# Two feed-forwards whose later blocks multiply with normed activations instead of norming the products

## The chip, the cores and the metric

The kernel runs on one core of a Trainium2 chip. The metric is the time of one execution in microseconds, the median of three runs. The kernel is one program for five engines, named as in the profile: PE (matrix products, with PEld for loading weights), DVE (vector work), ACT (activation functions and copies), POOL (GpSimd) and SP (which issues the weight transfers). Each engine works through its own list in order and waits on semaphores for what others make.

## The reference, cut to what matters

256 tokens of width 1024 go through a first block (feed-forward, attention mixers, feed-forward, a gate) and then through a second block of two layers. Each layer of the second block ends as follows, and the change lies in the gate and up products here:

```python
def swiglu_ffn(x, w_gate, w_up, w_down):
    return (jax.nn.silu(x @ w_gate) * (x @ w_up)) @ w_down

y = memory_cross_attention(x, mem_n, xa_wq[l], xa_wk[l], xa_wv[l], xa_wo[l])
x = layer_norm(ALPHA * x + y, ln_xa_g[l], ln_xa_b[l])
y = swiglu_ffn(x, ffn_wg[l], ffn_wu[l], ffn_wd[l])
x = layer_norm(ALPHA * x + y, ln_ffn_g[l], ln_ffn_b[l])
```

The hidden width of the feed-forward is 2816. Everything is float32.

## The kernel before, in words

Activations lie transposed: a tile holds 128 channels on the partitions and the 256 tokens along the free axis, so the 1024 channels are 8 tiles. A weight matrix is cut into 128x128 tiles, and an out block j is the sum over 8 weight tiles. The gate and up matrices are interleaved: even j is a gate block, odd j the up block beside it, 44 blocks for a layer. To keep float32 accuracy with fast products each operand is cut into a rounded part `hi` and a rest `lo`, and each weight tile takes three matmuls: weight hi by activation hi, weight hi by activation lo, weight lo by activation hi. The prediction calls these three a triple; a block is 8 triples.

Weights stream in units of 8 tiles. In `get`, called once a unit, ACT rounds the unit four ahead (L309, `hi<-raw`) and DVE makes the rest of the unit three ahead (L333, `lo<-raw,hi`, 128x1024). `get` also runs one step of a background generator, and `tick` runs the next step of every delayed piece of work. The lists of all engines are thus fixed by this one program, unit by unit; nothing is ordered again later.

The norm ahead of the feed-forward is deferred. While the sum z = ALPHA x + y of a channel tile comes out of the attention, `Norm.add` makes `xs`, which is z times the gain, in two parts, plus two further columns with gain and bias: 258 columns. The products of the gate and up blocks start on `xs` at once, before mean and variance are known. With a delay of two units the statistics are gathered, and in the fifth unit of the stage two tiles come ready, `rows`: the reciprocal deviation and minus the scaled mean, spread over the partitions. Blocks 0 to 3 wait in PSUM until then; the matmuls of block 4 come right behind the transposes that make `rows`. From then on each block is finished by `evac`: ACT copies the two further columns (L679), DVE multiplies the product by the one row (L680) and adds the other (L681); for a gate block ACT then takes Silu (L1896), for an up block DVE multiplies it with the gate (L1902), and the result is cut in two by ACT (L436) and DVE (L437).

The residual of the next norm needs the normed x itself. `Norm.values` makes it in the background, one channel tile k in three units: DVE multiplies z by the one row (L693) and adds the other (L694), ACT applies gain and bias (L696).

Line numbers here and in the rows are those of the kernel before; in the changed kernel the same lines stand 5 higher up to `Norm.values` (L680 is L685), 6 higher inside it, and 31 higher in the last of them (L1902 is L1933).

Of the kernel before, what the change touches and what calls it, by code (L numbers as in the profile page):

```python
# [9 lines left out]
F32 = mybir.dt.float32  # L10
F32R = mybir.dt.float32r
U32 = mybir.dt.uint32
AF = mybir.ActivationFunctionType
ALU = mybir.AluOpType
# [3 lines left out]
T = 256  # L18
D = 1024
NB = D // P  # L20
# [162 lines left out]
class Net:  # L183
    def __init__(self, tc=None, aps=None, order=None, dbg=None):
        self.dry = tc is None
        self.order = [] if self.dry else order
        self.packers = {}
        self.pos = 0
        self.prepped = 0
        self.rested = 0  # L190
        self.delayed = []
        self.eager = False
        self.half = {}
        self.loaded = 0
        self.ready = {}
        self.raws = {}
        self.bg = deque()
        self.dbg = dbg
        if self.dry:
            self.nc = self.tc = NULL  # L200
            self.aps = {k: NULL for k in ("xT", "pT", "memT", "vec0", "vec", "const", "bias", "wts", "out")}
            self.pe = self.ve = self.ac = self.po = NULL
        else:
            self.tc, self.nc, self.aps = tc, tc.nc, aps
            self.pe, self.ve, self.ac, self.po = (
                tc.nc.tensor, tc.nc.vector, tc.nc.scalar, tc.nc.gpsimd)
            self.chunks = chunks_of(order)
            self.chunk_of = {}
            for c, (units, _, _) in enumerate(self.chunks):
                for u in units:  # L210
                    self.chunk_of[u] = c
# [139 lines left out]
        for _ in self.gen_B(*a, **k):  # L351
            pass

    def gen_T(self, name, tiles, src, x, evac, w=T, whole=(), xf=None):


        left = {}
        for j, k in tiles:
            left[j] = left.get(j, 0) + 1
        seen = set()  # L360
        self.packers[name] = lambda inp, u: np.concatenate(
            [src(inp, j, k) for j, k in tiles[8 * u:8 * u + 8]], axis=1)
        acc = {}
        for t, (j, k) in enumerate(tiles):
            if t % 8 == 0:
                hi, lo = self.get(name, t // 8, P * min(8, len(tiles) - t), t // 8 in whole)
            if j not in acc:
                acc[j] = self.ps("acc")
            c = 128 * (t % 8)
            o = acc[j][:, :w]  # L370
            first, last = j not in seen, left[j] == 1
            seen.add(j)
            left[j] -= 1
            if t // 8 in whole:
                self.mm(o, hi[:, c:c + P], xf[k], start=first, stop=last)
            else:
                xk = x(k) if callable(x) else x[k]
                self.mm(o, hi[:, c:c + P], xk[:, :w], start=first, stop=False)
                self.mm(o, hi[:, c:c + P], xk[:, w:2 * w], start=False, stop=False)
                self.mm(o, lo[:, c:c + P], xk[:, :w], start=False, stop=last)  # L380
            if last:
                evac(j, o)
                del acc[j]
            if t % 8 == 7 or t + 1 == len(tiles):
                yield
# [251 lines left out]
class Norm:  # L637
# [5 lines left out]
    def __init__(self, net, name, off=0, delay=1, over=1.0):  # L643
        self.delay = delay
        self.net, self.g, self.b, self.off = net, name + "_g_2", name + "_b_2", off
        self.stats = Stats(net, NB, LN_EPS / over ** 2, True, TAIL_N)
        self.pend = None
        self.xs, self.keep = {}, {}

    def add(self, k, z):  # L650
        n, ve, ac, po = self.net, self.net.ve, self.net.ac, self.net.po
# [29 lines left out]
        ve.scalar_tensor_tensor(t, NM, c[:, 0:1], t, ALU.mult, ALU.add)  # L681
        return t, c[:, 1:2]

    def values(self, pace=1):

        n, ve, ac = self.net, self.net.ve, self.net.ac
        for k in range(NB):
            while not self.rows.ready:
                yield
            R, NM = self.rows.rb  # L690
            x = n.St("x")
            z = self.stats.z[k]
            ve.tensor_tensor(x, z, R, ALU.mult)  # L693
            ve.tensor_tensor(x, x, NM, ALU.add)  # L694
            g, b = n.vec(self.g, self.off + k), n.vec(self.b, self.off + k)
            n.later(lambda x=x, g=g, b=b: ac.activation(x, x, AF.Identity, scale=g, bias=b))  # L696
            self.keep[k] = x
            for _ in range(pace):
                yield

# [1156 lines left out]
def second_block(n, H, xs, KT, V, filler, lb):  # L1859
    ac, ve, po, pe = n.ac, n.ve, n.po, n.pe  # L1860

    def residual(X, norm, scale=None):
        def evac(j, o):
            z = n.St("z")
            if scale is None:
                ve.scalar_tensor_tensor(z, X[j], ALPHA, o, ALU.mult, ALU.add)  # L1866
            else:
                ve.scalar_tensor_tensor(z, o, scale[:, j:j + 1], X[j], ALU.mult, ALU.add)
            norm(j, z)
        return evac  # L1870

    X = {k: H[k] for k in range(NB)}
    for l in range(2):

        ln = Norm(n, "ln_mix", l * NB, D_MIX[l], ALPHA if l else 1.0)
        if l == 0:
            yo, late = hybrid(n, X, xs, filler, lb)
            late()
            n.stream_T("abo", row_tiles(NB, NB, A_HEAD), lambda inp, j, k: cut(w2(inp, "ab_w_out_2"), k, j),
                       yo, residual(X, ln.add))  # L1880
        else:
            sc = n.st("psc", 8)
            po.tensor_scalar(sc, n.vec("pool_scale_2", 0, NB), 1.0 / ALPHA, None, ALU.mult)
            pool_mixer(n, X, xs, residual(X, ln.add, sc), filler)
        filler.through(l)
        nx = Norm(n, "ln_xa", l * NB, D_XA)
        cross(n, l, ln, KT[l], V[l], residual(ln.keep, nx.add))
        X = ln.keep
        n.debug("mix%d" % l, [X[k] for k in range(NB)])
        ln = nx  # L1890
        hd, held = {}, {}

        def evac(j, o):
            t, c = ln.apply(o, "s", ac.copy)
            if j % 2 == 0:
                act = once(lambda: ac.activation(t, t, AF.Silu, bias=c))  # L1896
                n.later(act)
                held[j // 2] = t, act
            else:
                s, act = held.pop(j // 2)  # L1900
                act()
                ve.scalar_tensor_tensor(s, t, c, s, ALU.add, ALU.mult)  # L1902
                hd[j // 2] = n.split_later(s, name="hd")

        n.bg.append(ln.values(3))
        n.stream_T("g%d" % l, row_tiles(2 * NF, NB, G_HEAD),
                   lambda inp, j, k, l=l: cut(w2(inp, ("ffn_wg_2", "ffn_wu_2")[j % 2], l), k, j // 2),
                   ln.xs, ln.rows.after(evac), Norm.W)
        n.settle()
        n.flush_bg()  # L1910
        X = ln.keep
        n.debug("xa%d" % l, [X[k] for k in range(NB)])
        st = n.stats(NB, LN_EPS, True, TAIL_D[l])
        n.stream_T("d%d" % l, row_tiles(NB, NF), lambda inp, j, k, l=l: cut(w2(inp, "ffn_wd_2", l), k, j),
                   hd, residual(X, lambda j, z: st.add(z)))
        if l == 0:
            keep = {}
            for k in range(NB):
                keep[k] = n.St("xp", 272)
                po.memset(keep[k][:, 0:16], 0.0)  # L1920
            lz = Lazy(n, st, "ln_ffn_g_2", "ln_ffn_b_2", 0,
                      keep={k: keep[k][:, 16:272] for k in range(NB)})
            lz.start(lambda: filler.fill(F_POOL[0]))
            xs = (lz, keep)
            X = lz.keep
        else:
            rm = st.norm_cols()
            R, M, nm = n.ps("pb"), n.ps("pb"), n.St("nm")
            n.bcast(R[:, :T], rm)
            n.bcast(M[:, :T], rm[:, 2:4])  # L1930
            ac.copy(nm, M[:, :T])
            ts = {}

            def finish(k):
                add = po if k in POOL_ADDS else ve
                add.tensor_tensor(ts[k], ts[k], nm, ALU.add)
                x = n.St("x")
                ac.activation(x, ts[k], AF.Identity, scale=n.vec("ln_ffn_g_2", NB + k),
                              bias=n.vec("ln_ffn_b_2", NB + k))
                n.nc.sync.dma_start(out=n.aps["out"][:, k * T:(k + 1) * T], in_=x)  # L1940

            for k in range(NB):
                ts[k] = n.St("nt")
                ve.tensor_tensor(ts[k], st.z[k], R[:, :T], ALU.mult)
                if k > 1:
                    finish(k - 2)
            finish(NB - 2)
            finish(NB - 1)
# [128 lines left out]
```

## Time and profile before

| what | us |
|---|---|
| median of three runs | 1269.68 (1269.11 to 1271.19) |
| the profiled execution | 1269.32 |
| its span in the trace | 1267.4 |
| PE busy in the span | 1246.4 |
| DVE busy | 954.4 |
| ACT busy | 702.0 |
| POOL busy | 106.2 |

The 1.9 us between the execution's time and its span lie around the first and last instruction. A busy time is the union of an engine's instructions. A PE instruction's record lasts longer than the distance to the next one, since matmuls overlap; the pace is read from the starts. The two gate and up stages run from about 758 to 887 us and from about 1063 to 1191 us of the span.

### The profile page before, as it was taken

The numbers are of one execution on the slowest core, as the hardware profiler recorded it, in microseconds if no ns is written. First come the engines' busy times: TensorE is split into PE (matmuls) and PEld (weight loads), VectorE is DVE, ScalarE is ACT, GpSimd is POOL, SyncE is SP. The second block draws the span as 40 slices with busy tenths as digits, with TensorE's granted clock in tenths as the row PEclk, the third lists the DMA queues.
The fourth block names the chain that finished last, engine by engine and source line by source line (L and its number), as shares of the span: only waits on it lengthen the run. The fifth ranks groups of instructions, "written<-read, shape, count | busy, mean of one in ns | idle before, by whom it ended". The sixth has DMA issues, their size and how long they took to land.

```text
span 1267.4 us, 23973 instructions
## 1 busy us (share of the span) xinstructions
PE 1246.4 (98%) x9748; PEld 1206.7 (95%) x9748; DVE 954.4 (75%) x1749; ACT 702.0 (55%) x1269; POOL 106.2 (8%) x232
## 2 busy tenths in 40 slices
PE   8999999999999999999999999999999999999996
PEld 8999998879999999998889999999999899999996
DVE  6778656875766567679999778998558868998753
ACT  6656546566644454464466675655445676565532
POOL 1001002500000000000012120000003030000000
PEclk9999999999999999999999999999999999999998
DMA  8645555431455545544344334555544425355541
GB/s 295 224 170 205 202 182 194 156 128 67 167 180 187 191 177 198 195 172 150 116 167 167 133 127 146 198 197 191 209 167 162 172 101 200 130 194 179 203 161 34
DMA packets 32589, 215.15 MB, mean 170 GB/s; under 512 B 3872, under 2 KB 5152, under 8 KB 7776
## 3 DMA queue, kind: packets, MB, share of 16 engines
q1 hardware_dynamic: 31680, 211.28, 45.9%
q0 software_dynamic: 800, 2.36, 0.5%
q8 instruction: 76, 1.25, 0.4%
q14 instruction: 33, 0.27, 0.1%
HBM read 212.57 MB, written 1.05 MB: 169 GB/s over the span
## 4 chain that ended last, share of the span: by engine, by line
PE 92%; DVE 4%; ACT 2%; DMA 1%; issue 0%; POOL 0%; SPq 0%; ACTq 0%; DVEq 0%
PE acc L344 75%; PE accB L344 5%; PE vB L344 3%; PE kT L344 3%; PE S L344 1%; DVE lo L333 1%; DMA raw<-wts 1%; PE pv L344 1%; PE oM L344 1%; PE pt L992 1%; PE O L344 0%; ACT E L976 0%; ACT hi L309 0%; DVE sb L969 0%; PE ds L344 0%
## 5 line engine op out<-in xcount | busy, mean ns | idle before, releaser
L344 PE MATMUL acc<-xs,hi 128*128 128x256 f32 (+1 forms) x3392 | 613.3, 283 | 1.5 <-ACT hi L309 0.8
L344 PEld LDWEIGHTS acc<-xs,hi 128*128 128x128 f32 x3392 | 524.3, 189 | 2.6 <-ACT hi L309 1.1
L333 DVE TENSOR_TENSOR lo<-raw,hi 128x1024 fp32r<-128x1024 f32 (+2 forms) x395 | 472.2, 1211 | 10.0 <-ACT hi L309 9.5
L344 PE MATMUL acc<-xs,lo 128*128 128x256 f32 (+1 forms) x1696 | 478.4, 282 | 0.8 <-DVE lo L333 0.8
L309 ACT CAST hi<-raw 128x1024 fp32r<-128x1024 f32 (+2 forms) x395 | 403.2, 1039 | 35.9 <-DMA raw<-wts 14.1
L344 PEld LDWEIGHTS acc<-xs,lo 128*128 128x128 f32 x1696 | 322.6, 190 | 1.2 <-DVE lo L333 1.2
L344 PE MATMUL acc<-hd,hi 128*128 128x256 f32 x1408 | 249.6, 281 | 0.0
L344 PEld LDWEIGHTS acc<-hd,hi 128*128 128x128 f32 x1408 | 215.5, 188 | 0.0
L344 PE MATMUL acc<-hd,lo 128*128 128x256 f32 x704 | 197.2, 280 | 0.0
L344 PEld LDWEIGHTS acc<-hd,lo 128*128 128x128 f32 x704 | 132.6, 188 | 0.0
L344 PE MATMUL acc<-yo,hi 128*128 128x256 f32 x512 | 92.9, 283 | 0.3 <-ACT yo L443 0.2
L436 ACT CAST hd<-s 128x256 fp32r<-128x256 f32 x88 | 35.8, 407 | 103.4 <-DVE s L791 58.0
L344 PEld LDWEIGHTS acc<-yo,hi 128*128 128x128 f32 x512 | 78.9, 188 | 1.0 <-ACT yo L443 0.5
L344 PE MATMUL acc<-yo,lo 128*128 128x256 f32 x256 | 71.9, 281 | 0.0
L344 PE MATMUL accB<-hi,xs 128*128 128x512 f32 (+1 forms) x192 | 59.8, 393 | 0.0
L512 ACT ACTIVATE sq<-z 128x256 f32<-128x256 f32 x48 | 19.6, 407 | 68.7 <-DVE z L1866 68.7
L680 DVE TENSOR_TENSOR s<-acc,rows 128x256 f32<-128x256 f32 x88 | 37.0, 421 | 20.2 <-ACT c L679 20.2
L1866 DVE SCALAR_TENSOR_TENSOR z<-x,acc 128x256 f32<-128x256 f32 x32 | 13.2, 418 | 51.5 <-PE acc L344 51.5
L760 ACT ACTIVATE xs<-h,vt 128x256 fp32r<-128x256 f32 x24 | 12.2, 510 | 69.0 <-DVE h L803 66.9
L1573 DVE SCALAR_TENSOR_TENSOR cv<-up,vt,cv 128x256 f32<-128x256 f32 x120 | 50.0, 479 | 0.0
L344 PEld LDWEIGHTS acc<-yo,lo 128*128 128x128 f32 x256 | 48.2, 188 | 0.0
L589 POOL TENSOR_TENSOR r<-m,mhalf 128x2 f32<-128x2 f32 x8 | 12.0, 1503 | 420.9 <-DVE m L588 420.9
(306 smaller groups left out, 1479.9 us busy)
## 6 DMA issues: line engine op xcount, KB each, us to landing
raw<-wts SPq DMA_DIRECT2D x193, 1024.0 KB, 4.8
raw<-wts SPq DMA_DIRECT2D x6, 512.0 KB, 8.6
raw<-wts SPq DMA_DIRECT2D x2, 832.0 KB, 4.3
x<-xT SPq DMA_DIRECT2D x4, 256.0 KB, 6.5
mem<-memT POOLq DMA_DIRECT2D x8, 128.0 KB, 4.8
bias<-bias POOLq DMA_DIRECT2D x4, 256.0 KB, 3.1
out<-x SPq DMA_DIRECT2D x8, 128.0 KB, 1.9
raw<-wts SPq DMA_DIRECT2D x1, 768.0 KB, 4.1
```

The costliest lines, as they stand in the source:

```text
L309: self.ac.copy(hi[:, c], raw[:, c])
L333: self.ve.tensor_tensor(lo[:, c], raw[:, c], hi[:, c].bitcast(F32), ALU.subtract)
L344: self.pe.matmul(out, a, b, start=start, stop=stop, **k)
L436: self.later(lambda: self.ac.copy(hi, src), lambda: self.ve.tensor_tensor(xs[:, T:], src, hi.bitcast(F32), ALU.subtract))
L512: self.net.ac.activation(sq, z, AF.Square)
L589: net.po.tensor_tensor(r[:, 0:2], m[:, 2:4], net.mhalf[:, :2], ALU.pow)
L680: ve.tensor_tensor(t, o[:, :T], R, ALU.mult)
L760: ac.activation(hi, h, AF.Copy, scale=g)
L992: n.pe.transpose(o[:, kb * T + t * P:kb * T + (t + 1) * P], E[:, t * T + kb * P:t * T + (kb + 1) * P], n.ident)
L1573: ve.scalar_tensor_tensor(a, u[:, k:k + T], w, a, ALU.mult, ALU.add)
L1866: ve.scalar_tensor_tensor(z, X[j], ALPHA, o, ALU.mult, ALU.add)
```

## The change

`Norm.values` now works on POOL in the two feed-forwards (the attention keeps DVE), and one channel tile a unit instead of one in three. Behind it two more steps are queued for each tile: ACT rounds the normed x to `xn` hi (L706), and DVE makes its lo part (L709). Once all eight tiles have passed through the list, `pick` gives the next pair of blocks `xn` instead of `xs`: 256 columns, nothing to norm behind them. ACT then takes Silu straight from PSUM (L1919) and DVE multiplies from PSUM (L1922).

```diff
@@ Norm
-    def values(self, pace=1):
+    def values(self, split=False):
         n, ve, ac = self.net, self.net.ve, self.net.ac
+        add = n.po if split else ve
         for k in range(NB):
             while not self.rows.ready:
                 yield
...
-            ve.tensor_tensor(x, z, R, ALU.mult)
-            ve.tensor_tensor(x, x, NM, ALU.add)
+            add.tensor_tensor(x, z, R, ALU.mult)
+            add.tensor_tensor(x, x, NM, ALU.add)
             g, b = n.vec(self.g, self.off + k), n.vec(self.b, self.off + k)
-            n.later(lambda x=x, g=g, b=b: ac.activation(x, x, AF.Identity, scale=g, bias=b))
+            steps = [lambda x=x, g=g, b=b: ac.activation(x, x, AF.Identity, scale=g, bias=b)]
+            if split:
+                xn = n.Tt("xn", F32R)
+                hi = xn[:, :T]
+                steps.append(lambda x=x, hi=hi: ac.copy(hi, x))
+                def low(x=x, hi=hi, xn=xn, k=k):
+                    ve.tensor_tensor(xn[:, T:], x, hi.bitcast(F32), ALU.subtract)
+                    self.normed[k] = xn
+                steps.append(low)
+            n.later(*steps)
             self.keep[k] = x
-            for _ in range(pace):
-                yield
+            yield
+    def pick(self, j):
+        if j % 2 == 0:
+            self.late = len(self.normed) == NB
+        return (self.normed, T) if self.late else (self.xs, self.W)
@@ second_block
         def evac(j, o):
+            if late[j]:
+                if j % 2 == 0:
+                    s = held[j // 2] = n.St("s")
+                    ac.activation(s, o, AF.Silu)
+                else:
+                    s = held.pop(j // 2)
+                    ve.tensor_tensor(s, s, o, ALU.mult)
+                    hd[j // 2] = n.split_later(s, name="hd")
+                return
             t, c = ln.apply(o, "s", ac.copy)
...
-        n.bg.append(ln.values(3))
+        n.bg.append(ln.values(True))
```

In the list of PE the new operand begins with block 14 in both layers, so that 30 of the 44 blocks are 256 columns wide. The last rows of block 13 and the first of block 14 in the first layer, before:

```order
L344 MATMUL acc_9774<-xs_9193,hi_9614 128x258 x2
L344 MATMUL acc_9774<-xs_9193,lo_9656 128x258
L344 MATMUL acc_9774<-xs_9235,hi_9614 128x258 x2
L344 MATMUL acc_9774<-xs_9235,lo_9656 128x258
L344 MATMUL acc_9817<-xs_9018,hi_9654 128x258 x2
L344 MATMUL acc_9817<-xs_9018,lo_9694 128x258
```

The same six rows now, where `xn_9460` is the normed tile k = 0:

```order
L344 MATMUL acc_9817<-xs_9193,hi_9635 128x258 x2
L344 MATMUL acc_9817<-xs_9193,lo_9684 128x258
L344 MATMUL acc_9817<-xs_9235,hi_9635 128x258 x2
L344 MATMUL acc_9817<-xs_9235,lo_9684 128x258
L344 MATMUL acc_9857<-xn_9460,hi_9682 128x256 x2
L344 MATMUL acc_9857<-xn_9460,lo_9726 128x256
```

No matmul has moved; the operand and the width have changed.

On DVE the piece around the evacuation of blocks 12 and 13 of the same layer stood before as follows; `lo_9735` is the rest of unit 15, `lo_9770` of unit 16, `lo_9813` of unit 17, and `acc_9738` and `acc_9774` are blocks 12 and 13:

```order
L333 TENSOR_TENSOR lo_9735<-raw_9498,hi_9692 128x1024
L680 TENSOR_TENSOR s_9763<-acc_9738,rows_9395 128x256
L681 SCALAR_TENSOR_TENSOR s_9763<-rows_9395,c_9764,s_9763 128x256
L333 TENSOR_TENSOR lo_9770<-raw_9576,hi_9733 128x1024
L437 TENSOR_TENSOR hd_9730<-s_9684,hd_9730 128x256
L680 TENSOR_TENSOR s_9799<-acc_9774,rows_9395 128x256
L681 SCALAR_TENSOR_TENSOR s_9799<-rows_9395,c_9800,s_9799 128x256
L1902 SCALAR_TENSOR_TENSOR s_9763<-s_9799,c_9800,s_9763 128x256
L693 TENSOR_TENSOR x_9806<-z_9061,rows_9395 128x256
L694 TENSOR_TENSOR x_9806<-x_9806,rows_9395 128x256
L333 TENSOR_TENSOR lo_9813<-raw_9576,hi_9768 128x1024
```

Now the rests of the normed tiles 5, 6 and 7 (`xn_9679`, `xn_9723`, `xn_9768`) stand between them; blocks 12 and 13 are `acc_9779` and `acc_9817`, and the rests of units 16 and 17 are `lo_9811` and `lo_9853`:

```order
L709 TENSOR_TENSOR xn_9679<-x_9676,xn_9679 128x256
L685 TENSOR_TENSOR s_9804<-acc_9779,rows_9395 128x256
L686 SCALAR_TENSOR_TENSOR s_9804<-rows_9395,c_9805,s_9804 128x256
L333 TENSOR_TENSOR lo_9811<-raw_9591,hi_9771 128x1024
L709 TENSOR_TENSOR xn_9723<-x_9720,xn_9723 128x256
L442 TENSOR_TENSOR hd_9764<-s_9715,hd_9764 128x256
L685 TENSOR_TENSOR s_9842<-acc_9817,rows_9395 128x256
L686 SCALAR_TENSOR_TENSOR s_9842<-rows_9395,c_9843,s_9842 128x256
L1933 SCALAR_TENSOR_TENSOR s_9804<-s_9842,c_9843,s_9804 128x256
L333 TENSOR_TENSOR lo_9853<-raw_9591,hi_9809 128x1024
L709 TENSOR_TENSOR xn_9768<-x_9765,xn_9768 128x256
```

The pair L693, L694 is gone from this list (POOL has it), one L709 has come for each tile, and the rest of the eighth tile stands behind the whole evacuation of block 13 and behind the rest of unit 17.

## Rows read from the trace of the kernel before

**Rows 1.** Page, busy time of each engine, share of the span, instructions.
```profile
PE 1246.4 (98%) x9748; PEld 1206.7 (95%) x9748; DVE 954.4 (75%) x1749; ACT 702.0 (55%) x1269; POOL 106.2 (8%) x232
```
**Rows 2.** Chain that ended last, in order: start, us, engine, tile, line, count.
```profile
770.42 178.64 PE acc L344 x1488
...
1075.13 178.68 PE acc L344 x1488
```
**Rows 3.** Windows: stretch, its length, busy time by engine, PE clock, DMA.
```profile
783.00:800.00 17.00, 17.00 (x143) 17.00 (x142) 16.61 (x30) 10.48 (x23) 0.00 (x0) 1.00 0.52 186
```
**Rows 4.** Timeline of PE: start, duration, instruction (x2: two merged).
```profile
781.89 0.41 PE L344 MATMUL acc<-xs,hi 128*128 128x258 f32 x2
782.14 0.28 PE L344 MATMUL acc<-xs,lo 128*128 128x258 f32 x1
...
799.33 0.40 PE L344 MATMUL acc<-xs,hi 128*128 128x258 f32 x2
...
818.82 0.29 PE L344 MATMUL acc<-xs,lo 128*128 128x258 f32 x1
...
829.72 0.28 PE L344 MATMUL acc<-xs,lo 128*128 128x258 f32 x1
...
1219.88 0.28 PE L344 MATMUL acc<-hd,lo 128*128 128x256 f32 x1
...
1239.69 0.28 PE L344 MATMUL acc<-hd,lo 128*128 128x256 f32 x1
```
**Rows 5.** Timeline of DVE around the rest of unit 8.
```profile
779.55 0.49 DVE L681 SCALAR_TENSOR_TENSOR s<-rows,c,s 128x256 f32<-128x256 f32 x1
779.95 0.42 DVE L693 TENSOR_TENSOR x<-z,rows 128x256 f32<-128x256 f32 x1
780.41 0.42 DVE L694 TENSOR_TENSOR x<-x,rows 128x256 f32<-128x256 f32 x1
780.75 1.22 DVE L333 TENSOR_TENSOR lo<-raw,hi 128x1024 fp32r<-128x1024 f32 x1
781.89 0.42 DVE L680 TENSOR_TENSOR s<-acc,rows 128x256 f32<-128x256 f32 x1
...
795.73 0.42 DVE L693 TENSOR_TENSOR x<-z,rows 128x256 f32<-128x256 f32 x1
```
**Rows 6.** Timeline of DVE at the evacuation of block 13.
```profile
802.50 0.42 DVE L437 TENSOR_TENSOR hd<-s,hd 128x256 fp32r<-128x256 f32 x1
802.83 0.42 DVE L680 TENSOR_TENSOR s<-acc,rows 128x256 f32<-128x256 f32 x1
...
803.80 0.48 DVE L1902 SCALAR_TENSOR_TENSOR s<-s,c 128x256 f32<-128x256 f32 x1
804.21 0.42 DVE L693 TENSOR_TENSOR x<-z,rows 128x256 f32<-128x256 f32 x1
...
805.00 1.22 DVE L333 TENSOR_TENSOR lo<-raw,hi 128x1024 fp32r<-128x1024 f32 x1
```
**Rows 7.** Timeline of POOL: a cast beside a `lo`, and the kernel's end.
```profile
960.31 1.25 POOL L657 CAST xs<-vt 128x1 fp32r<-128x1 f32 x1
...
1258.73 0.72 POOL L1936 TENSOR_TENSOR nt<-nt,nm 128x256 f32<-128x256 f32 x1 [1.40 <-ACT nm L1931]
1260.48 0.85 POOL L1936 TENSOR_TENSOR nt<-nt,nm 128x256 f32<-128x256 f32 x1 [1.02 <-DVE nt L1944]
```
**Rows 8.** Timeline of DVE beside rows 7 (`pb` lies in PSUM).
```profile
960.30 1.22 DVE L333 TENSOR_TENSOR lo<-raw,hi 128x1024 fp32r<-128x1024 f32 x1
...
1258.84 0.90 DVE L1936 TENSOR_TENSOR nt<-nt,nm 128x256 f32<-128x256 f32 x1
...
1260.32 0.41 DVE L1936 TENSOR_TENSOR nt<-nt,nm 128x256 f32<-128x256 f32 x1
1260.66 0.41 DVE L1944 TENSOR_TENSOR nt<-z,pb 128x256 f32<-128x256 f32 x1
1260.99 0.62 DVE L1936 TENSOR_TENSOR nt<-nt,nm 128x256 f32<-128x256 f32 x1
```

More of the change, by code (lines that the diff above doesn't have):

```diff
@@ L352, in stream_B, with gen_T @@
             pass
-    def gen_T(self, name, tiles, src, x, evac, w=T, whole=(), xf=None):
+    def gen_T(self, name, tiles, src, x, evac, w=T, whole=(), xf=None, pick=None):
         left = {}
@@ L362, in gen_T @@
             [src(inp, j, k) for j, k in tiles[8 * u:8 * u + 8]], axis=1)
-        acc = {}
+        acc, picked = {}, {}
         for t, (j, k) in enumerate(tiles):
@@ L368, in gen_T @@
                 acc[j] = self.ps("acc")
+                if pick is not None:
+                    picked[j] = pick(j)
+            if pick is not None:
+                x, w = picked[j]
             c = 128 * (t % 8)
@@ L647, in __init__ @@
         self.pend = None
-        self.xs, self.keep = {}, {}
+        self.xs, self.keep, self.normed, self.late = {}, {}, {}, False
     def add(self, k, z):
@@ L1890, in second_block @@
         ln = nx
-        hd, held = {}, {}
+        hd, held, late = {}, {}, {}
         def evac(j, o):
+            if late[j]:
[7 more added lines that the diff above has]
+                return
             t, c = ln.apply(o, "s", ac.copy)
@@ L1903, in evac, with pick @@
                 hd[j // 2] = n.split_later(s, name="hd")
-        n.bg.append(ln.values(3))
+        def pick(j):
+            x, w = ln.pick(j)
+            late[j] = w == T
+            return x, w
+        n.bg.append(ln.values(True))
         n.stream_T("g%d" % l, row_tiles(2 * NF, NB, G_HEAD),
                    lambda inp, j, k, l=l: cut(w2(inp, ("ffn_wg_2", "ffn_wu_2")[j % 2], l), k, j // 2),
-                   ln.xs, ln.rows.after(evac), Norm.W)
+                   None, ln.rows.after(evac), pick=pick)
         n.settle()
```

## The prediction, made before the result was known

> **What bounds the kernel now.** I read the page first, then the chain that ended last, then the two gate and up stages in the timelines of PE and DVE, and at last the places where POOL and DVE work side by side.
>
> The page says that PE is busy for 98% of the span and DVE for 75% [rows 1]. The reader should not stop there: a mean over the span hides which engine a stage hangs on. The chain shows that both stages concerned are PE alone: 1488 matmuls in one piece of 178.64 us in the first layer and of 178.68 us in the second, with no wait in them [rows 2]. Those pieces hold 40 gate and up blocks and 20 of down products. So each nanosecond taken from a matmul there is won, and each wait put into PE's list there is lost.
>
> The second thing to see is that PE's freedom from waits hangs on a thread early in the stage. Between 783 and 800 us DVE is busy for 16.61 of 17.00 us [rows 3]. It is behind, because blocks 0 to 3 all had to wait for `rows`. How far behind, two places tell. Block 8 begins at 781.89 and uses the rest of its weights first at 782.14 [rows 4]; DVE finishes that rest at 780.75 + 1.22 = 781.97 [rows 5]. That is 0.17 us in hand. (That this is block 8: the piece of the chain starts with block 4, and four blocks of 8 triples on, at 0.3633 us a triple, is 11.63 us later, 782.05 by the chain; PE's record is 0.16 us ahead, since the chain counts the first triple only from the end of the transposes.) And block 13 has been multiplied out when block 14 begins at 799.33 [rows 4], but DVE starts to evacuate it only at 802.83 [rows 6]: 3.5 us behind PE. Before the change this lag costs nothing, since nothing on PE waits for an evacuation while PSUM has room.
>
> **Term 1, the narrower matmuls.** With 258 columns, 30 triples go from 818.82 to 829.72, 363.3 ns each. With 256 columns (the down products) 56 triples go from 1219.88 to 1239.69, 353.8 ns each [rows 4]. The difference is 9.5 ns for a triple. The order shows 30 late blocks in each layer: 30 x 8 = 240 triples, 2.28 us a layer. Nothing hides it; it all counts.
>
> **Term 2, the hand-over at block 14.** This block needs all eight `xn`. Its eighth triple is the first to read tile 7, and the second matmul of that triple reads the part that DVE makes (L709). With no wait PE would reach it at 799.33 + 7 x 0.354 + 0.12 = 801.93. On DVE, L709 of tile 7 stands behind the whole evacuation of block 13 and behind the rest of unit 17, as the order shows. When does it get there? By the list, until the end of that evacuation three pairs L693, L694 have gone (they start at 779.95 [rows 5], one between, and 795.73 [rows 5]), each worth 780.75 - 779.95 = 0.80 us, 2.40 together. Seven L709 have come. The like operation L437 takes 802.83 - 802.50 = 0.33 us of the queue [rows 6], so 2.3 together. DVE is then where it was: free behind L1902 at 804.21 [rows 6]. Then the rest of unit 17, which takes 781.89 - 780.75 = 1.14 us of the queue [rows 5], and L709 itself, 0.42: done at 805.77. With less than 0.1 for the semaphore PE has waited from 801.93 to about 805.83, 3.9 us. The lag that was free is now paid, because a matmul waits for the last thing in the lagging queue.
>
> Behind block 14 I see no further wait: the evacuation of a late pair costs DVE one operation from PSUM and ACT one Silu in place of two copies, five vector operations and a Silu.
>
> **Term 3, POOL beside DVE.** POOL gets 16 operations on 128x256 tiles, two a channel tile, in one run from 771 us on, since all their inputs are there once `rows` is. At its end the kernel has two of the same kind: 0.72 us with no such DVE operation ahead of it, and 0.85 [rows 7]. At 1258.84 DVE's L1936, with both inputs in SBUF, began under the first and took 0.90 us in place of the 0.41 at 1260.32; at 1260.99, under the second, 0.62. But L1944, with one input in PSUM, took its 0.41 in the midst of the second [rows 8]. Worked back from DVE's ends (1259.74 - 0.41 = 1259.33), POOL held DVE off for 0.60 us from its own start the first time; the second hold, from 1261.33 - 0.72 = 1260.61 (a POOL operation of 0.72 that ended at 1261.33 and had waited 0.13 for DVE) to 1261.61 - 0.41 = 1261.20, is 0.59. The reverse is there as well: a POOL cast at 960.31 took 1.25 us beside a `lo` that ran from 960.30 for 1.22 [rows 7, 8]. So each keeps the other out, whoever comes first, if DVE reads two SBUF tensors.
>
> DVE's list from 771 us on is nearly all of that kind (L681, L1902, L437, L333); only L680 reads PSUM. I lay the two queues side by side, POOL entering whenever DVE's operation ends. L680 starts together with a POOL operation and takes 0.46 of its 0.59, so the L681 behind it waits 0.13: seven times, 0.9. L1902 comes behind L681, 0.52 after its start against 0.40 for the end of its hold, with a POOL operation slipped in at 0.40: 0.59 - 0.12 = 0.47 lost, less what POOL's own start takes, 0.44, three times, 1.3. The rests of units 8 and 9 lose a whole 0.59 each, 1.2. The rest of POOL's time falls into gaps in which DVE waits for ACT anyway. Together 3.4 us until POOL is through, near 788 us.
>
> PE meets the first part of it at block 8: ahead of the rest of unit 8 stand five L681, two L1902 and its own 0.59, 2.1 us; it comes at 781.97 - 0.80 (the pair before it is gone) + 2.1 = 783.3, wanted at 782.14, a wait of about 1.1, and another 0.8 at block 9. What is left goes on with DVE's queue to block 14. Wherever it shows, all 3.4 get to PE, since L709 of tile 7 is the end of the same queue. The bounds: nothing, if the two do not meet, and 16 x 0.59 = 9.4 if each POOL operation stops DVE in full. I take 3.4, because the end's rows show both cases, DVE stopped and DVE passing on PSUM inputs.
>
> The Trainium skill has a rule that speaks against this step: "SBUF — State Buffer", section "Who interferes with whom", says that a VectorE instruction with two SBUF inputs contends with a GpSimd instruction that reads SBUF, that one with at most one SBUF input doesn't, and that the later of the two is blocked for the whole instruction. By that rule, the trace agrees in kind (0.90 for 0.41, and 0.41 for the one with PSUM); and held for the whole 0.72 rather than 0.59 it would add 0.13 at each of the 12 places, 1.6 a layer, and make the time 1282.5.
>
> **What costs nothing.** ACT gains eight casts and loses 30 copies; it is busy for 10.48 of 17 us [rows 3], and hands the weights over four units ahead. The pace of one tile a unit in place of three sets no end: the normed x are wanted only in the down products.
>
> **Sum.** Per layer 3.9 + 3.4 - 2.28 = 5.0, for two layers 10.0 us. On the profiled execution, 1269.32 (span 1267.4 and 1.9 around it), that is 1279.3; its own time is 0.36 under the median of the runs, which would make 1279.7. I say 1279.3.
>
> **Rivals.** First, hand-over without the clash: POOL and DVE pass each other, term 3 is nothing. Then 2 x (3.9 - 2.28) = +3.2, 1272.5. For it: L1944 was not touched by POOL. Against it: L1936 was, twice, and DVE's list is of its kind. 15 in 100.
>
> Second, the clash in full: 9.4 a layer, 2 x (3.9 + 9.4 - 2.28) = +22, 1291.4. For it: the rests of 1.14 us are long, and one lost place in the queue could bring a second; against it: POOL has spare time in DVE's own gaps, and L680 passes. 9 in 100.
>
> Third, faster: the hand-over costs PE nothing, because DVE has caught up by block 14. Then only term 1 stays: 1269.3 - 4.6 = 1264.7. For it: eight pairs leave DVE. The point from which it decides is the end of L709 of tile 7: before 801.93 there is no wait, and up to 804.2 the layer still comes out level. Against it: only three of the pairs lie ahead of that point, and seven L709 take their place; DVE would have to gain 3.9 us, or 1.6 for no loss, with no gaps in its list. 7 in 100.
>
> That the change does not do what it says (no late blocks) is ruled out by the order, which has 480 triples on `xn`.
>
> **Chances and range.** The forecast holds 64 in 100, with its own range 1276 to 1284 (term 3 between 1.8 and 5.8 us a layer); 5 in 100 are left for a time within the noise by a shorter lag. The range of 1272 to 1286 takes in the forecast and the first rival. A measurement of this kernel tells a change of about 0.2%, 2.5 us, from none. Slower is the forecast and the first two rivals, 0.64 + 0.15 + 0.09 = 0.88 (the first lies just beyond that bound); same is the 5 in 100 and one of the third rival's 7, 0.06; faster is the other 0.06.
>
> **What would show it.** In the trace after: PE waits near 782 us for `lo` of L333, and at block 14, near 802 us, for L709, in both layers, the second the larger; late triples at 353.8 ns; the sixteen POOL operations between 771 and 788 us, some of them longer than 0.72; L681, L1902 and L333 longer than 0.48, 0.48 and 1.22 in that stretch and nowhere else. Wrong it would be if PE's piece from 770 us still ran through without a wait, or if L709 of tile 7 ended before 802 us.

## The result, and the profile after

The changed kernel takes 1281.84 us (median of 4 runs, 1281.25 to 1281.94), the kernel before 1270.43 beside it (4 runs, 1269.11 to 1272.18). The ratio is 1.0088, with a 95% interval of 1.0072 to 1.0104: slower by 11.4 us, where 10.0 and a time of 1279.3 were forecast. The profiled execution of after took 1281.94 with a span of 1280.1, 12.7 more than the span before. The head of the page of after, which answers to [rows 1]:

```profile
PE 1247.0 (97%) x9748; PEld 1205.4 (94%) x9748; DVE 898.2 (70%) x1613; ACT 694.0 (54%) x1225; POOL 135.7 (11%) x264
```

DVE has lost 56 us of work, ACT 8, POOL has gained 30, and the kernel is slower. PE does the same 9748 matmuls in about the same busy time; what has grown is its idle time. PE's waits, with the total, their number and the longest:

```profile
PE acc L344 <- DVE xn L709: 8.5, 4, 2.6
...
PE acc L344 <- DVE lo L333: 2.1, 6, 0.8
```

The first row is new: two matmuls in each layer wait for the part of `xn` that DVE makes. Waits for `lo` have become six, where there was one of 0.8 us. In the chain of waits of after the unbroken pieces of [rows 2] have come apart:

```profile
764.60 5.81 PE acc L344 x48
...
781.36 1.69 DVE lo L333
...
808.59 148.20 PE acc L344 x1226
...
1016.51 5.77 PE acc L344 x48
...
1076.57 5.80 PE acc L344 x48
...
1120.41 146.41 PE acc L344 x1226
1266.83 1.69 PE tot L344 x16
```

From 771.57 us, when `rows` is there, to the end of L709 at 808.54 the chain of the first layer runs through DVE, with ACT's small steps between, and no row of PE stands in it: when L709 comes is set by DVE's queue and not by PE. PE itself waits at three places, for the rests of the weights of blocks 8 and 9 and at the hand-over at block 14. To see what each costs I measure each layer from the 48 matmuls ahead of `rows`: the first layer to the next 48 of the kind, the second to the matmuls of the statistics behind its last block (`tot`). The rows of before for these places:

```profile
764.17 5.81 PE acc L344 x48
...
1008.85 5.81 PE acc L344 x48
...
1068.87 5.82 PE acc L344 x48
...
1253.81 1.69 PE tot L344 x16
```

In the first layer that was 244.68 us before (764.17 to 1008.85) and is 251.91 (764.60 to 1016.51), 7.23 more; the second layer goes from 184.94 (1068.87 to 1253.81) to 190.26 (1076.57 to 1266.83), 5.32 more. What lies between the two is unchanged (60.02 and 60.06). So the loss is in these two stages, and is not alike in both.

PE's timeline at the three places (in brackets the idle time before an instruction and what ended it) is the answer to [rows 4]:

```profile
783.09 0.39 PE L344 MATMUL acc<-xs,lo 128*128 128x258 f32 x1 [0.38 <-DVE lo L333]
...
786.53 0.39 PE L344 MATMUL acc<-xs,lo 128*128 128x258 f32 x1 [0.26 <-DVE lo L333]
...
800.92 0.40 PE L344 MATMUL acc<-xn,hi 128*128 128x256 f32 x2
...
805.41 0.39 PE L344 MATMUL acc<-xn,hi 128*128 128x256 f32 x1 [1.70 <-DVE xn L709]
...
808.59 0.58 PE L344 MATMUL acc<-xn,hi 128*128 128x256 f32 x1 [2.56 <-DVE xn L709]
808.97 0.42 PE L344 MATMUL acc<-xn,lo 128*128 128x256 f32 x1
...
809.61 0.41 PE L344 MATMUL acc<-xn,lo 128*128 128x256 f32 x1
...
819.79 0.28 PE L344 MATMUL acc<-xn,lo 128*128 128x256 f32 x1
...
834.77 0.28 PE L344 MATMUL acc<-xn,lo 128*128 128x256 f32 x1
...
1129.97 0.28 PE L344 MATMUL acc<-xn,lo 128*128 128x256 f32 x1
...
1144.77 0.28 PE L344 MATMUL acc<-xn,lo 128*128 128x256 f32 x1
```

Blocks 8 and 9 wait a little, block 14 long. From the 48 matmuls to block 14 it was 799.33 - 764.17 = 35.16 us, and is 800.92 - 764.60 = 36.32: 1.16 went on blocks 8 and 9. Without a wait the second matmul on tile 7 would come at 800.92 + 7 x 0.357 + 0.12 = 803.54; it comes at 808.59, 5.05 later. (The idle times in brackets, 1.70 and 2.56, are less, since a matmul's record goes on after the next could have begun.) Now look at the rows behind it: at 808.97 and 809.61 two triples begin 0.64 us apart. Ten microseconds on, 42 triples from 819.79 to 834.77 take 0.357 each, and in the second layer 42 from 1129.97 to 1144.77 take 0.352. The reason stands in the windows, whose column before the last two is the clock that PE was granted:

```profile
804.00:806.00 2.00, 0.59 (x3) 0.42 (x3) 2.00 (x4) 1.48 (x3) 0.00 (x0) 1.00 0.77 315
806.00:808.00 2.00, 0.03 (x1) 0.00 (x0) 1.93 (x4) 0.40 (x1) 0.00 (x0) 0.81 0.42 176
808.00:810.00 2.00, 1.41 (x6) 1.41 (x7) 2.00 (x4) 0.58 (x2) 0.00 (x0) 0.50 0.28 41
...
814.00:816.00 2.00, 2.00 (x19) 2.00 (x18) 1.52 (x3) 0.41 (x1) 0.00 (x0) 0.98 0.03 8
```

While PE stands still for tile 7 its clock falls from 1.00 to 0.50 (from 2.4 to 1.2 GHz), and it is back only in the window from 814 us. Until then each triple takes 0.64 us. The wait at block 14 is paid twice, and the second part appears in no row of waits, since PE is busy. DVE's timeline shows what it waits for, the answer to [rows 5, 6]:

```profile
774.24 0.84 DVE L1933 SCALAR_TENSOR_TENSOR s<-s,c 128x256 f32<-128x256 f32 x1
...
781.28 1.76 DVE L333 TENSOR_TENSOR lo<-raw,hi 128x1024 fp32r<-128x1024 f32 x1
...
784.72 1.75 DVE L333 TENSOR_TENSOR lo<-raw,hi 128x1024 fp32r<-128x1024 f32 x1
...
805.61 0.42 DVE L685 TENSOR_TENSOR s<-acc,rows 128x256 f32<-128x256 f32 x1
...
...
806.98 1.22 DVE L333 TENSOR_TENSOR lo<-raw,hi 128x1024 fp32r<-128x1024 f32 x1
808.12 0.42 DVE L709 TENSOR_TENSOR xn<-x,xn 128x256 fp32r<-128x256 f32 x1
```

L709 of tile 7 is the last row. Ahead of it stand, in the order forecast, the evacuation of block 13 and the rest of unit 17. The three longer rows lie early, where POOL runs:

```profile
771.55 0.74 POOL L699 TENSOR_TENSOR x<-z,rows 128x256 f32<-128x256 f32 x1 [2.13 <-ACT c L684]
...
781.15 0.81 POOL L700 TENSOR_TENSOR x<-x,rows 128x256 f32<-128x256 f32 x1
781.92 1.71 POOL L699 TENSOR_TENSOR x<-z,rows 128x256 f32<-128x256 f32 x1
...
785.47 1.59 POOL L700 TENSOR_TENSOR x<-x,rows 128x256 f32<-128x256 f32 x1
```

Sixteen such rows reach from 771.55 to 787.06. The first takes 0.74 us, beside an L685 with one input in PSUM (0.72 in [rows 7]), and the longest 1.71, beside a `lo`; DVE's `lo` takes 1.76 in place of 1.22 [rows 5] there, and L1933 0.84 in place of 0.48.

### The profile page after: what moved, and what is told of

The parts are those of the page before. It is cut to its first block, busy times and chain, and to the rows that moved or that the text cites. A ratio compares the mean times of both kernels' runs of the same rounds, so it can differ in the third digit from the quotient of the medians.

```text
span 1280.1 us, 23825 instructions
## 1 busy us (share of the span) xinstructions
PE 1247.0 (97%) x9748; PEld 1205.4 (94%) x9748; DVE 898.2 (70%) x1613; ACT 694.0 (54%) x1225; POOL 135.7 (11%) x264
## 4 chain that ended last, share of the span: by engine, by line
PE 86%; DVE 9%; ACT 3%; issue 1%; DMA 1%; POOL 0%; SPq 0%; ACTq 0%; DVEq 0%
PE acc L344 69%; PE accB L344 5%; PE vB L344 3%; PE kT L344 3%; DVE lo L333 3%; PE S L344 1%; DVE s L686 1%; DVE s L685 1%; DVE s L1933 1%; DMA raw<-wts 1%; PE pv L344 1%; PE oM L344 1%; PE pt L1014 1%; PE O L344 0%; ACT E L998 0%
## 5 line engine op out<-in xcount | busy, mean ns | idle before, releaser
L344 PE MATMUL acc<-xs,hi 128*128 128x256 f32 (+1 forms) x2432 | 437.6, 282 | 3.3 <-ACT hi L309 2.6
L344 PEld LDWEIGHTS acc<-xs,hi 128*128 128x128 f32 x2432 | 374.4, 189 | 4.5 <-ACT hi L309 3.0
L344 PE MATMUL acc<-xs,lo 128*128 128x256 f32 (+1 forms) x1216 | 342.5, 282 | 2.1 <-DVE lo L333 2.1
L344 PEld LDWEIGHTS acc<-xs,lo 128*128 128x128 f32 x1216 | 230.1, 189 | 3.4 <-DVE lo L333 3.4
L344 PE MATMUL acc<-xn,hi 128*128 128x256 f32 x960 | 176.1, 285 | 8.8 <-DVE xn L709 8.5
L344 PEld LDWEIGHTS acc<-xn,hi 128*128 128x128 f32 x960 | 151.3, 193 | 10.0 <-DVE xn L709 10.0
L344 PE MATMUL acc<-xn,lo 128*128 128x256 f32 x480 | 136.8, 285 | 0.0
L344 PEld LDWEIGHTS acc<-xn,lo 128*128 128x128 f32 x480 | 92.3, 192 | 0.0
L1922 DVE TENSOR_TENSOR s<-s,acc 128x256 f32<-128x256 f32 x30 | 12.6, 422 | 82.5 <-PE acc L344 82.5
```

Source lines behind the costliest of these rows:

```text
L344: self.pe.matmul(out, a, b, start=start, stop=stop, **k)
L1922: ve.tensor_tensor(s, s, o, ALU.mult)
```

## The experiments

In the diffs + marks the kernel run and - the changed kernel. First I asked where the loss lies, by doing less of the change.

**The late blocks from 16 on.** The wait should go if block 14 does not read `xn` yet.

```
-            self.late = len(self.normed) == NB
+            self.late = len(self.normed) == NB and j >= 16
```

> One number is changed: the later blocks use the normed activations from block 16 on, not from block 14; POOL, ACT and DVE do the same work in the same order up to there. Hand-over theory: the loss sits in PE's wait at block 14 (about 5.1 us a layer in the trace after) and in the lower PE clock behind that wait (about 2.5 and 1.9 us). Two blocks later the rest of tile 7 is ready before PE asks for it (808.5 against about 809.3 us), so both go; left are the waits at blocks 8 and 9 (1.2 us a layer) against 28 x 8 triples that are 7 to 10 ns shorter (about 1.9 us): 1.5 us under before, 1269 us, no PE wait at block 16, granted clock 1.00 all through the stage. Rival, POOL's clash with DVE carries the loss: the clash is unchanged, so the time stays near 1281. Rival, the 256-column blocks themselves or their evacuation cost it: near 1281 as well, 28 of 30 blocks being left.

Measured: 1267.81 (11 runs) against 1269.57, ratio 0.9989 (0.998 to 0.9998). The wait for L709 is gone and the clock stays at 1.00; the chain of the first layer runs through PE alone from block 9 on:

```profile
786.54 162.79 PE acc L344 x1366
```

DVE's list is the same, but PE comes later:

```profile
808.12 0.42 DVE L709 TENSOR_TENSOR xn<-x,xn 128x256 fp32r<-128x256 f32 x1
```

It ends at 808.54, and block 16 needs it near 809.3 (block 14's start, 800.9, 16 triples of 0.363, 7 of 0.357 and 0.12). The layers stand at -0.26 and -1.66 us against before. Two blocks later turn a loss of 7.23 and 5.32 into a small gain: the hand-over is the cause of the slowdown. What is left is consistent with a wait of about 1 us at blocks 8 and 9 less 28 x 8 narrower triples.

**POOL alone.** POOL makes the normed x, but no `xn` is made, and all blocks are 258 wide.

```
-            if split:
+            if False:
```

> One part of the change alone: the normed x are made on POOL, one tile a unit, but no rounded parts are made and all blocks stay 258 columns wide with the norm behind. Hand-over theory with the clash as a lesser term: PE waits at blocks 8 and 9 for the rest of the weights, 1.2 us a layer, and nowhere else in the stage: about 2.3 us over before, 1272.7 us; L1933 of 0.48 and the rests of units 8 and 9 of 1.22 us take 0.84 and 1.75 us. Rival, no clash: DVE only loses work, time as before, 1270.4. Rival, the clash carries the loss: 5 us or more a layer, over 1280.

Measured: 1272.88 (8 runs), ratio 1.0022 (1.0011 to 1.0032); the layers +1.08 and +1.02. So POOL beside DVE costs something by itself, at blocks 8 and 9:

```profile
784.92 0.39 PE L344 MATMUL acc<-xs,lo 128*128 128x258 f32 x1 [0.36 <-DVE lo L333]
```

It is 1.1 us of what DVE loses; the rest stays in DVE's lag, which nothing on PE waits for in this kernel.

**DVE in place of POOL.** The other way round: all of the change, with the 16 operations of a layer on DVE.

```
-        add = n.po if split else ve
+        add = ve
```

> The whole change but for POOL: the normed x are made on DVE as before, one tile a unit, and block 14 is still the first late one. Hand-over theory: the rest of tile 7 stands at the end of DVE's queue, which now holds eight pairs of 0.80 us (6.4) in place of 3.4 us of clash; it comes 3.0 us later, so PE waits 3.0 us a layer more, and the time is about 6 us above the changed kernel, 1288 us. Rival, the clash carries the loss: with POOL out of it the time falls to 1275 or below.

Measured: 1289.3 (5 runs), ratio 1.0157 (1.0143 to 1.0171); the layers +11.17 and +9.09, so 3.94 and 3.77 more than with POOL (3.0 was expected, with 3.4 for the clash). L709 of tile 7 now comes at the end of a list that is longer by eight pairs:

```profile
813.44 0.42 DVE L709 TENSOR_TENSOR xn<-x,xn 128x256 fp32r<-128x256 f32 x1
```

This weighs the clash. Eight pairs take 8 x 0.80 = 6.4 us of DVE's queue; by giving them to POOL the change has won 3.9 at block 14. The difference, 2.5, is what POOL takes from DVE; the longer rows of after, summed below, say 2.4.

**PE kept busy.** Does the fall of the clock cost what the slow triples say, or is it only the wait seen again? This kernel does additional matmuls in block 14, 14 ahead of triple 6 and 20 ahead of triple 7, into a spare PSUM tile that nothing reads.

```
+                if pick is not None and j == 14 and k in FILL:   # FILL = {6: 14, 7: 20}
+                    fill = self.ps("fill")
+                    for i in range(FILL[k]):
+                        self.mm(fill[:, :w], hi[:, c:c + P], x[0][:, :w], start=(i == 0), stop=(i + 1 == FILL[k]))
```

> The changed kernel with PE kept at work during its wait: 14 matmuls ahead of the seventh and 20 ahead of the eighth triple of block 14 (256 columns, into a PSUM tile that nobody reads, about 1.65 and 2.4 us at 118 ns each, less than the waits of 1.9 and 2.7 us there). The data are ready no sooner. If the lower granted clock behind the wait (0.50 for some 5 us in both layers) comes from PE's idling, it stays at 1.00, the triples of block 15 take 354 and not 640 ns, and the time falls by 2.5 and 1.9 us, to about 1277.5 us. If the clock falls for another reason, or costs nothing, the time stays at 1281.8 or grows.

Measured: 1279.43 (5 runs), ratio 1.0078 (1.0065 to 1.009). Timeline of PE at block 14:

```profile
803.71 1.84 PE L345 MATMUL fill<-xn,hi 128*128 128x256 f32 x14
...
806.03 2.55 PE L345 MATMUL fill<-xn,hi 128*128 128x256 f32 x20
...
808.87 0.39 PE L345 MATMUL acc<-xn,hi 128*128 128x256 f32 x1 [0.18 <-DVE xn L714]
809.10 0.28 PE L345 MATMUL acc<-xn,lo 128*128 128x256 f32 x1
```

Windows of the same kernel:

```profile
808.00:812.00 4.00, 3.82 (x32) 3.61 (x32) 2.29 (x4) 2.27 (x3) 0.00 (x0) 1.00 0.59 199
```

Chain of the same kernel:

```profile
808.87 145.76 PE acc L345 x1226
...
1118.91 144.52 PE acc L345 x1226
```

The matmul on tile 7 comes as late as in after, but the next one follows within 0.23 us, at a clock of 1.00. The pieces of 1226 matmuls are shorter by 148.20 - 145.76 = 2.44 and 146.41 - 144.52 = 1.89 us: the price of the clock, apart from the wait. The whole gains less than the 4.3 of the pieces: 2.4 us by medians, and the intervals of the two ratios overlap (1.0088 and 1.0078), so that the total alone would not show it. Between the profiled executions the spans differ by 3.4 us (1280.1 and 1276.7), and the layers by 1.72 and 1.94. About 0.7 of the first layer's gain is lost again in the attention behind the stage (from 974.58 to 1015.08, 40.50 us, where after has 39.78, 976.73 to 1016.51). I can place neither the cause of that nor the rest.

Then I asked whether the change can be had without its costs, by holding POOL back until DVE has caught up. A copy of one column of a later block's tile on POOL, ahead of the sixteen, does that; late blocks begin two later than in after's rule.

**POOL behind block 8, and behind block 6.**

```
-            while not self.rows.ready:
+            while not self.rows.ready or (split and not self.open):
-            self.late = len(self.normed) == NB
+            self.late, self.full = self.full, len(self.normed) == NB
+            if j == 8:
+                po.tensor_copy(n.st("gate", 2)[:, 0:1], t[:, 0:1])
+                ln.open = True
```

(The line that sets `open` and `full` to False at the start is left out here.)

> Both waits are taken away at once. POOL starts its sixteen operations only after DVE has begun to evacuate block 8 (a copy of one column of that block's tile on POOL comes first), when the rests of the weights have two units more in hand, and the blocks change to the normed activations one pair after all eight tiles stand in the list: 24 late blocks a layer. Theory (hand-over, clash and clock): DVE still loses some 3 us to POOL, but its queue is waited for by nobody then, so PE runs through the stage without a wait and at clock 1.00; left is the gain of 24 x 8 triples, 6.6 ns each in the first layer and 10.9 in the second, 1.3 and 2.1 us: 3.4 us under before, 1266.2 us. Rival, what POOL takes from DVE reaches PE wherever it stands: 2 x (3.3 - 1.7), 3 us over before.

The second has 6 for 8.

> As the run gated at block 8, but POOL starts after block 6, with 26 late blocks a layer. Theory: 26 x 8 triples give 1.4 and 2.3 us; the rests of units 10 and 11 have about 2 us in hand and lose one POOL operation each and what stands ahead of them, so PE waits 0 to 0.5 us a layer: 2.7 to 3.7 us under before, 1266 to 1267 us. Rival as there: some 3 us over before.

Measured: 1272.28 (11 runs) against 1269.47, ratio 1.0023 (1.0014 to 1.0033), and 1273.85 (5 runs), 1.0035 (1.0022 to 1.0048). Both expectations failed; the time of the first one's rival came, 2.8 us over before where it had 3. Timeline of ACT of the one with 8:

```profile
790.81 0.51 ACT L1931 ACTIVATE s<-s,c 128x256 f32<-128x256 f32 x1 [1.76 <-POOL gate L1928]
792.52 0.60 ACT L703 ACTIVATE x<-x,vt 128x256 f32<-128x256 f32 x1 [1.19 <-POOL x L701]
793.02 0.14 ACT L685 COPY c<-acc 128x2 f32<-128x2 f32 x1
```

The timeline of DVE of the same kernel shows who waits for that copy:

```profile
793.20 0.42 DVE L686 TENSOR_TENSOR s<-acc,rows 128x256 f32<-128x256 f32 x1 [2.13 <-ACT c L685]
```

And the timeline of PE, who waits for DVE:

```profile
804.65 0.39 PE L344 MATMUL acc<-xs,lo 128*128 128x258 f32 x1 [1.68 <-DVE lo L333]
```

Block 8's tile is overwritten in place by ACT's Silu, which must wait until POOL has copied from it (1.76), and right behind, ACT waits for the first x of POOL (1.19). ACT works in order: the small copy L685 stands behind both, DVE waits 2.13 for it, and PE 1.68 for DVE at 804.65. The gate made a new wait. In both layers PE waits 1.68 us and, a block later, another 0.25 or 0.27: 1.9 in all, less than the 2.13 for which DVE stood still, so by these rows (an estimate) neither would have come without the standstill. But POOL's clash takes time from DVE in the same stretch, as the rival has it, and this run does not part the two. The one with 6 shows the same wait of 1.75 for its gate.

**More `lo` ahead.** The late blocks from 16 on, and `LOOK_LO = 4` in place of 3, so that DVE starts each rest a unit earlier and blocks 8 and 9 might not wait.

> As the run that switches at block 16, but DVE makes the rests of the weights four units ahead in place of three, everywhere in the kernel. The rest of unit 8 then stands ahead of the four pent-up evacuations and not behind them. Theory: the waits at blocks 8 and 9 (1.2 us a layer, all that was left of the change's cost) go, POOL's clash with DVE is met by a queue that nobody waits for, and the time falls by 2.3 us from that run, to 4 us under before, 1265.5 us. Rival, DVE is the bound in that stretch and the earlier rest only moves the wait to a later block: no better than that run, 1267.8 us, or worse.

Measured: 1306.79 (5 runs), ratio 1.0296 (1.0281 to 1.0311); failed. DVE now asks for the halves of ACT before they are there. Its waits:

```profile
DVE lo L333 <- ACT hi L309: 165.1, 135, 2.7
```

Before, that row had 9.5 us in 13 waits. It is so in the whole kernel: the 48 matmuls of the first layer come at 795.62 in place of 764.17, 31 of some 37 us lost ahead of the stage. Within the two stages, though, the theory came true. PE does not wait at blocks 8 and 9 in either layer, although the two `lo` there take 1.77 and 1.75 us beside POOL as before; PE's waits for `lo` in the whole kernel are down to two, and neither lies in these stages:

```profile
PE acc L344 <- DVE lo L333: 1.2, 2, 0.8
```

What is left has moved to block 16, where PE waits 0.67 and 0.16 us for L709. From the 48 matmuls of the first layer to the first products behind the stage it is 186.21 us (795.62 to 981.83), where the late blocks from 16 on have 187.12 (764.62 to 951.74). So the earlier rest takes the waits away, and costs far more in the rest of the kernel.

**POOL behind block 9, ACT's steps later.** The gate reads block 9's tile, which no Silu overwrites, and ACT's steps on x come two units later, so that ACT doesn't wait.

```
+            if j == 9:      # in place of 8
-            n.later(*steps)
+            n.later(*[lambda: None] * (2 if split else 0), *steps)
```

The rest is as behind block 8.

> The gated run again without what went wrong there by the trace: ACT stood still for 1.8 and 1.2 us, since its Silu had to wait until POOL's gate had read the tile that Silu overwrites, and its first step on the normed x was next in its list before POOL had made it; DVE waited 2.1 us behind it and PE 1.9 us for DVE. Now the gate reads the tile of block 9, which nobody overwrites, and ACT's steps come two units later; 20 late blocks a layer. Theory: those standstills were the cause, PE does not wait in the stage, and 20 x 8 triples give 1.1 and 1.7 us: 2.8 us under before, 1266.7 us. Rival: in the middle of the stage DVE's list has no gaps, so the clash alone (sixteen operations at about 0.5 us) makes PE wait for the rests of the weights: 2 us or more over that, 1269 to 1273 us.

Measured: 1267.14 (11 runs) against 1269.83, ratio 0.9979 (0.9971 to 0.9988), with 20 late blocks a layer; the layers -1.21 and -1.41. This beats both kernels. That it beats the late blocks from 16 on (0.9989) is not shown, since their intervals overlap. POOL's first row and DVE's `lo` beside POOL, by the timeline and by the view that groups instructions:

```profile
793.45 0.19 POOL L1928 COPY gate<-s 128x1 f32<-128x1 f32 x1 [22.77 <-DVE s L687]
```

```profile
L333 DVE TENSOR_TENSOR lo<-raw,hi 128x1024 fp32r<-128x1024 f32 x6 | 10.5, 1757 | 0.0
```

POOL still takes its half microsecond from each of the six `lo` that it meets, 6 x 0.54 = 3.2 us from these alone, more than it took from all of DVE's rows in after (2.4, below). But it comes some 21 us later in the stage (27.60 us behind the 48 matmuls in place of 6.95), where the rests of the weights have time in hand: the one that DVE starts at 793.83 is done at 795.58, and PE wants it at 798.34, 2.8 us later; block 8's had 0.17 before the change. That time is just used up. PE waits once in each layer, for 0.2 us, in the first layer here:

```profile
816.03 0.39 PE L344 MATMUL acc<-xs,lo 128*128 128x258 f32 x1
```

(the rest that it reads is done at 815.98). But for that the chain runs through PE alone from 772.10 us to the end of the stage. It is not the clash that costs time, but the place at which it comes. Against the run behind block 8 three things have changed at once, the gate's tile, POOL's start one block later and ACT's steps; what each is worth is not shown.

## Why the prediction was right, and where its sizes were off

The direction and the places were right, and so was the mechanism but for one term that it lacked. By its terms, in us for a layer:

| | forecast | first layer | second layer |
|---|---|---|---|
| waits at blocks 8 and 9 | 1.9 | 1.16 | 0.99 |
| wait at block 14 | 5.4 | 5.05 | 5.10 |
| slow triples after it | 0 | 2.44 | 1.89 |
| narrower triples | -2.28 | -1.58 | -2.62 |
| sum | 5.0 | 7.07 | 5.36 |
| measured | | 7.23 | 5.32 |

The second layer's waits are taken as the first's: 1112.72 - 1076.57 = 36.15 less 35.16, and 1120.41 - 1115.31.

**Term 2, the hand-over, right.** The queue named was the queue found: block 13's evacuation, the rest of unit 17, L709. DVE's L709 of tile 7 was put at 805.77 without the clash. With the 0.43 us by which the stage begins later and the clash's 2.4 it would be 808.60, and it ended at 808.54. The late blocks from 16 on show the same from the other side. The point from which the third rival decides was stated as L709's end before 804.2 for a level layer; it came 4.3 us after it.

**Term 3, the clash, too big by 1.0.** 3.4 was forecast, and DVE lost 2.4: two `lo` of 0.54 each (1.76 - 1.22), three L1933 of 0.36, and seven L686 of at most 0.07. The step that was off is the part of POOL's hold that reaches DVE. The prediction let a `lo` lose the whole 0.59, an L1902 0.44 and an L681 0.13; they lost 0.54, 0.36 and at most 0.07. So the seven come to some 0.3 in place of 0.9, the three to 1.1 in place of 1.3, the two to 1.1 in place of 1.2. A hold of 0.54 would give about these figures (0.54 less the 0.46 of L685 is 0.08), but the rows don't tell a shorter hold from one that began earlier: POOL's operation at 781.15 began 0.13 ahead of the `lo` at 781.28. And L685, with one input from PSUM, took its 0.42 as forecast. The Trainium skill ("SBUF — State Buffer", "Who interferes with whom") has whichever starts first hold the shared port pair for its whole instruction, with the other blocked. The trace agrees in kind: when that `lo` began, POOL's operation had 781.15 + 0.81 - 781.28 = 0.68 us to run by the records, and `lo` lost 0.54, somewhat less; the measurement decides. The first rival (no clash) was excluded by POOL alone, which waits at blocks 8 and 9 in both layers; the second (a clash of 9.4) by the same 2.4.

**Term 1, the narrower matmuls, off by layer.** 9.5 ns were taken from the down products' pace. The late triples took 356.7 ns in the first layer and 352.4 in the second, 6.6 and 10.9 ns less than 363.3: 1.58 and 2.62 for 240, which together is 4.20 in place of 4.56.

**A term was missing.** I took the cost of a wait to be its length. PE was idle but for three matmuls from 804 to 806 us, the last of which ended just behind 806, and the clock fell, which made the wait dearer by 2.44 and 1.89 us. No row that I had chosen shows PE standing for several microseconds within a stage, so the sum had no place for it. The overestimate of term 3 hides part of it: without the clock the two layers would have lost 4.63 and 3.47, less than the 5.0 forecast; with it the whole lies 2.5 us above the 1279.3. That the time came so near is in part luck: two misses of opposite sign.

One reading of the prediction that no sum rests on was off: the pieces of 1488 matmuls hold 40 gate and up blocks (960) and 528 matmuls of down products, which is 22 times 8 triples and not 20.

## What to carry to other kernels

An engine's lag behind another costs nothing until something waits for the end of its queue. Before a block is made to read a new tile, compare the time at which PE wants the last such tile with the end of the queue that makes it; two blocks' delay turned +0.9% into -0.1%. Price a wait of several microseconds on PE at its length and the slow matmuls behind it, and put work for POOL where what DVE makes has time in hand before PE wants it, not where POOL's inputs are first ready.

## What the runs showed of the hardware

- PE's granted clock fell to 0.50 in a wait of 5 us that three matmuls broke up, and triples took 0.64 us in place of 0.357 until 814 us, some 5 us after PE was busy again. Idle times of 0.38 and 0.26 us at blocks 8 and 9 didn't lower it, and 34 additional matmuls put into the long wait kept it at 1.00.
- The pace of 256-column triples on `xn` is 352 to 357 ns and differs between the layers of one kernel: 356.7 and 352.4 in after, the same to 0.2 ns in the late blocks from 16 on, in DVE in place of POOL and in PE kept busy, and 352.5 and 354.0 in the last experiment. Those of 258 columns took 363.1 to 363.5 in before and in POOL alone. `xn` lies in other buffers in these kernels; whether that is the cause was not tried.
- A tensor operation of POOL and one of DVE with both inputs in SBUF cost each other: DVE's `lo` 0.54 us (1.22 to 1.76), POOL's 0.74 grew to 1.71.
